# Fourth mixer: the state-space maps and the rotary scores of two heads placed side by side on TensorE's array

## The chip, the cores and the metric

The kernel runs on one NeuronCore of a Trainium2 chip. The metric is the device time of one launch in microseconds (us). PE is TensorE, DVE is VectorE, ACT is ScalarE, POOL is GpSimd, SP is the engine that issues most DMAs. All times below are of one core.

## The reference, cut to what matters

The program is six blocks in a row over 512 positions of width 1024: two mixers of one network, then a second network with mixer, FFN, mixer, FFN. The change lies in the last mixer (the "fourth"), which adds a state-space layer (S5) and latent attention (MLA) side by side:

```python
def odd_mixer_2(t, w_in, ...):
    proj = t @ w_in                      # u (256), c_q (256), c_kv (128), k_r (64)
    y_c = s5_ssm(u, ...)                 # 16 groups of 16 channels, 64 complex states each
    y_d = mla_attention(c_q, c_kv, k_r, ...)   # 6 heads
    return concatenate([y_c, y_d], -1) @ w_out

def s5_ssm(u, ...):
    bu_re = einsum('bsgh,gph->bsgp', ug, bb_re)
    bu_im = einsum('bsgh,gph->bsgp', ug, bb_im)
    x = scan over s of  x_s = ab * x_(s-1) + bu_s        # complex
    y = einsum(x_re, c_re) - einsum(x_im, c_im) + d_skip * ug
    z = gelu(y);  return z * sigmoid(z @ w_glu + b_glu)

def mla_attention(...):
    # per head: 128 plain + 64 rotary columns of q; the rotary key is one for all heads
    sc = (q_nope . k_nope + q_rope . k_rope) * scale
    p = softmax(where(chunk_causal_mask, sc, -inf));  return p @ v
```

## The kernel before, in words

One core runs a single stream of instructions per engine. A framework with tile pools orders each engine's stream when the program is built, by priorities and its own due times; on the chip every stream runs in that order, and a semaphore holds an instruction until what it needs is there. PSUM is eight banks in four pools: P (two banks), Z (three), W (two), O (one). SBUF work tiles come from a pool of 14 tiles of 128x2048 values (`A4`) and one of 13 rows (`U`).

The fourth mixer is `odd2` (line 967). Its stages in order:

- `projT("o2t", ...)` makes `uT`, the 256 S5 channels on partitions: `uT[:, 0]` and `uT[:, 1]`. `projS("o2s", ...)` makes the latents for each of four row blocks; `lat` (line 985) normalises them and transposes them into `CT` and `krT`.
- keys and queries (`kn`, `qn`, lines 1069 to 1087), the rotary part of the queries (`qrT`, up to line 1101) and the values (`va`, line 1108) follow.
- The S5 layer has 8 state tiles. `s5(j, t)` (line 1012) loads a rotation table `tab`, runs two matmuls of 32 contraction rows, `bur` and `bui` (line 1020), and then 14 DVE instructions of 512 columns (lines 1024 to 1033, two of them scans), which end in `sa` (real, line 1030) and `yi` (imaginary, line 1033). `s5_out` (line 1038) maps them to 32 output columns with two matmuls into `py` (lines 1043 and 1044); after four tiles, line 1047 makes `yg`. `s5_step` runs `s5_out` for a tile when the next tile has been written. The tiles 0 to 2 stand before the attention (banks Z), the other five between its heads (banks P).
- `attn(hd)` (line 1116) runs one head: for the four row blocks 1, 2, 3, 0 (256, 384, 512, 128 columns) a plain score matmul of 128 rows (line 1123) and a rotary one of 64 rows (line 1124) into one Z bank `sc`, then `softmax_rows` (memset of the masked corner, DVE maximum, ACT exponential, lines 407 to 411), a DVE reciprocal, an ACT scaling, PE transposes `pw` and an ACT copy into `wt` (line 352). `av2` multiplies by the values (`po`, line 1138).
- The gate of S5 (`zs`, `pp`, `g`, lines 1157 to 1173) ends in `mix(0)` and `mix(1)`, which the output projection `outp` takes last of its eight pieces. `outp` (line 285) also splits the output weights on ACT and DVE (`wb`, `wl`, lines 132 and 115) and adds into eight banks `y`.

Every matmul from FP32 data (scores, `bur`, `bui`, `py`, `po`, transposes over 128 columns aside) is two PE instructions in the trace. In the loop over heads the order is `attn(hd)`, `s5_step(1)`, so one state tile stands beside each head:

Of the kernel before, what the change touches and what calls it, by code (L numbers as in the profile page):

```python
# [12 lines left out]
AF = mybir.ActivationFunctionType  # L13
# [37 lines left out]
class Net:  # L51
# [830 lines left out]
    def s5_setup(self):  # L882
# [61 lines left out]
        for ri in range(2):  # L944
            V.tensor_tensor(w[0], bc[:, ri], b8(fre), ALU.mult)
            V.tensor_tensor(w[1], bc[:, 1 - ri], b8(fim), ALU.mult)
            V.tensor_tensor(w[2], w[0], w[1], ALU.subtract if ri == 0 else ALU.add)
            for jj in range(2):
                pt = self.bank("W", "pbb")
                for c in range(4):  # L950
                    self.nc.tensor.matmul(pt[32 * c : 32 * c + 32, 0:P], lhsT=w[2][:, 4 * jj + c], rhs=self.ident, start=True, stop=True)
                nc.scalar.copy(self.bbT[:, jj, ri], pt[:, 0:P])
# [17 lines left out]
    def odd2(self):  # L970
# [41 lines left out]
        def s5(j, t):  # L1012
            jj, c = j // 4, j % 4
            rs = slice(32 * c, 32 * c + 32)
            tab = self.A4(name="tab")[:, 0:2]
# [3 lines left out]
            for ri, pp in ((0, pr), (1, pi)):  # L1019
                nc.tensor.matmul(pp, lhsT=self.bbT[rs, jj, ri], rhs=uT[rs, jj], start=True, stop=True)  # L1020
            rb = self.rho[:, j : j + 1].to_broadcast([P, S])
            yr, yi, a, b = (self.U(name=n) for n in ("yr", "yi", "sa", "sb"))
            for o, p0, p1, op in ((yr, pr, pi, ALU.add), (yi, pi, pr, ALU.subtract)):
                V.tensor_tensor(a, p0, ct_, ALU.mult)
                V.tensor_tensor(b, p1, st_, ALU.mult)
# [4 lines left out]
            V.tensor_tensor(a, a, b, ALU.subtract)  # L1030
            V.tensor_tensor(yr, yr, st_, ALU.mult)
            V.tensor_tensor(yi, yi, ct_, ALU.mult)
            V.tensor_tensor(yi, yr, yi, ALU.add)
            return a, yi

        py = {}

        def s5_out(j, xr, xi):
            jj, c = j // 4, j % 4
            if c == 0:  # L1040
                py[jj] = self.bank("O", "py")
# [17 lines left out]
        self.s5n = 0  # L1059
        s5_step(1, "Z")  # L1060
# [7 lines left out]
        with self.prio(300):  # L1068
            kn = [self.A4(name="kn") for _ in range(2)]
            qn = [self.A4(name="qn") for _ in range(2)]  # L1070
            va = [self.A4(name="va") for _ in range(2)]
            qrT = self.A4(name="qrT")
            h, l = self.wload("o2kv", 0, 768)
            for hd in range(6):
                ps = self.pb()
                c = slice(hd * P, hd * P + P)
                self.mm3(ps, (h[:, c], l[:, c]), ct(2), True, True)
                nc.scalar.copy(kn[hd // 4][:, hd % 4], ps)
            for pc in range(2):
                h, l = self.wload("o2q", pc, 768)  # L1080
                hv, lv = (t.rearrange("p (k h c) -> p k h c", k=2, h=3) for t in (h, l))
                for g in range(3):
                    hd = 3 * pc + g
                    ps = self.pb()
                    for k in range(2):
                        self.mm3(ps, (hv[:, k, g], lv[:, k, g]), ct(k), k == 0, k == 1)
                    nc.scalar.activation(qn[hd // 4][:, hd % 4], ps, AF.Copy, scale=MLA_SC)
            h, l = self.wload("o2q", 2, 768)
# [26 lines left out]

        def attn(hd):
            r = slice(64 * (hd % 2), 64 * (hd % 2) + 64)
            q, k = qn[hd // 4][:, hd % 4], kn[hd // 4][:, hd % 4]
            wt = self.A4(name="wt")
            for tb in (1, 2, 3, 0):  # L1120
                N = (tb + 1) * P
                ps = self.bank("Z", "sc")
                nc.tensor.matmul(ps[:, :N], lhsT=q[:, tb * P : N], rhs=k[:, :N], start=True, stop=False)  # L1123
                nc.tensor.matmul(ps[:, :N], lhsT=qrT[r, hd // 2, tb * P : N], rhs=krT[r, :N], start=False, stop=True)  # L1124
                e, sm = self.softmax_rows(ps, N)
                rr = self.st(1, "rr")
                V.reciprocal(rr, sm)
                nc.scalar.activation(e[:, :N], e[:, :N], AF.Copy, scale=rr)
                flush()
                self.evac_wt(wt, e, tb)  # L1130
            todo.append(lambda: av2(hd, wt))

# [259 lines left out]
```

## Time and profile before

| | us |
|---|---|
| time, median of three runs (lowest, highest) | 1715.97 (1713.16, 1719.6) |
| the profiled execution's own time | 1708.09 |
| span of the profiled execution | 1706.3 |
| PE busy | 1657.1 (97%) |
| PE weight loads busy | 1318.5 (77%) |
| DVE busy | 964.3 (57%) |
| ACT busy | 669.6 (39%) |
| stretch of the fourth mixer spoken of here | about 1137 to 1340 |

The busy shares are averages over six blocks with different limits. A PE instruction's record is longer than the step to the next one, because matmuls are pipelined; steps between starts are what a stretch costs. Where a view merges several instructions into one row, `x4` is their number.

### The profile page before, as it was taken

How to read it: one execution, taken by the hardware profiler on the slowest of the kernel's cores; microseconds unless marked ns; L12 is line 12 of the kernel's file. 1: busy time of each engine (PE TensorE's matmuls, PEld its weight loads, DVE VectorE, ACT ScalarE, POOL GpSimd, SP SyncE). 2: the span in 40 equal slices, each digit the busy share in tenths (PEclk: the TensorE clock that was granted, in tenths of full speed). 3: DMA queues.
4: the chain of work that ended last, by engine and by line, in shares of the span. 5: the costliest groups of instructions: out<-in, count | busy, mean ns of one | idle time of the engine just before them, and what ended most of it. 6: DMA issues, size and time to landing. Idle time of an engine off the chain costs nothing. (4 is left out here: it accounts for less than half of the span.)

```text
span 1706.3 us, 20536 instructions
## 1 busy us (share of the span) xinstructions
PE 1657.1 (97%) x8008; PEld 1318.5 (77%) x8008; DVE 964.3 (57%) x1824; ACT 669.6 (39%) x1174; POOL 2.0 (0%) x8
## 2 busy tenths in 40 slices
PE   8999999999999998699999999999999999999998
PEld 8657788988789875588888888886447988888886
DVE  7564456765676998763222278468695622224332
ACT  5554234214545246543222244344456422224231
POOL 0000000000000000000000000000000000000000
PEclk8999999999999999799999999999999999999999
DMA  5212243202153220152223235432005323222341
GB/s 204 84 38 74 80 179 117 72 29 99 62 198 115 74 84 1 65 195 101 98 99 99 99 118 196 170 126 78 25 25 197 112 99 99 99 98 89 97 161 50
DMA packets 50241, 175.06 MB, mean 103 GB/s; under 512 B 5584, under 2 KB 6096, under 8 KB 50016
## 3 DMA queue, kind: packets, MB, share of 16 engines
q1 hardware_dynamic: 40896, 142.20, 24.6%
q10 hardware_dynamic: 9216, 31.48, 4.9%
q8 instruction: 63, 1.03, 0.3%
q14 instruction: 34, 0.28, 0.1%
q0 software_dynamic: 32, 0.07, 0.0%
HBM read 156.95 MB, written 16.78 MB: 102 GB/s over the span
## 5 line engine op out<-in xcount | busy, mean ns | idle before, releaser
L115 DVE TENSOR_TENSOR wl<-wr,wh 128x1024 fp32r<-128x1024 f32 (+2 forms) x224 | 271.3, 1213 | 350.4 <-ACT wh L132 335.4
L132 ACT CAST wh<-wr 128x1024 fp32r<-128x1024 f32 (+2 forms) x224 | 233.0, 1042 | 534.8 <-PE pp L147 409.8
L147 PE MATMUL pp<-xl,wh 128*128 128x512 f32 (+1 forms) x1184 | 428.1, 362 | 0.2 <-DVE xl L115 0.2
L144 PE MATMUL pp<-xh,wh 128*128 128x512 f32 (+1 forms) x1184 | 425.2, 361 | 1.2 <-ACT xh L234 1.2
L148 PE MATMUL pp<-xh,wl 128*128 128x512 f32 (+1 forms) x1184 | 425.3, 360 | 0.0
L144 PEld LDWEIGHTS pp<-xh,wh 128*128 128x128 f32 x1184 | 223.6, 190 | 36.1 <-ACT xh L234 2.5
L147 PEld LDWEIGHTS pp<-xl,wh 128*128 128x128 f32 x1184 | 224.4, 190 | 34.0 <-DVE xl L115 1.2
L148 PEld LDWEIGHTS pp<-xh,wl 128*128 128x128 f32 x1184 | 224.4, 190 | 33.7 <-issue 2.3
L147 PE MATMUL pp<-wl,xh 128*128 128x512 f32 (+1 forms) x320 | 126.9, 396 | 0.0
L148 PE MATMUL pp<-wh,xl 128*128 128x512 f32 (+1 forms) x320 | 125.9, 394 | 0.0
L144 PE MATMUL pp<-wh,xh 128*128 128x512 f32 (+1 forms) x320 | 125.9, 393 | 0.0
L144 PE MATMUL y<-wh,ah 128*128 128x512 f32 x288 | 112.5, 390 | 0.0
L147 PE MATMUL y<-wl,ah 128*128 128x512 f32 x288 | 112.3, 390 | 0.0
L148 PE MATMUL y<-wh,al 128*128 128x512 f32 x288 | 112.2, 389 | 0.0
L1189 DVE TENSOR_TENSOR act<-g,pp 128x512 f32<-128x512 f32 x44 | 30.2, 687 | 132.9 <-PE pp L148 131.5
L750 DVE SCALAR_TENSOR_TENSOR ycv<-up,vec,ycv 128x512 f32<-128x512 f32 x120 | 84.4, 740 | 0.4
L144 PEld LDWEIGHTS pp<-wh,xh 128*128 128x128 f32 x320 | 60.2, 188 | 13.9 <-issue 2.6
L147 PEld LDWEIGHTS pp<-wl,xh 128*128 128x128 f32 x320 | 60.2, 188 | 12.9 <-issue 2.4
L148 PEld LDWEIGHTS pp<-wh,xl 128*128 128x128 f32 x320 | 60.3, 188 | 11.1 <-issue 0.6
L321 DVE TENSOR_TENSOR yn<-y,nw 128x512 f32<-128x512 f32 x48 | 31.8, 685 | 58.0 <-ACT yn L319 52.2
L144 PEld LDWEIGHTS y<-wh,ah 128*128 128x128 f32 x288 | 54.1, 188 | 11.5 <-issue 0.4
L148 PEld LDWEIGHTS y<-wh,al 128*128 128x128 f32 x288 | 54.1, 188 | 11.1
(373 smaller groups left out, 2314.0 us busy)
## 6 DMA issues: line engine op xcount, KB each, us to landing
wr<-in_f0gu SPq DMA_DIRECT2D x44, 512.0 KB, 3.3
wr<-in_f1gu SPq DMA_DIRECT2D x44, 512.0 KB, 3.3
wr<-in_f0d SPq DMA_DIRECT2D x22, 512.0 KB, 3.4
wr<-in_f1d SPq DMA_DIRECT2D x22, 512.0 KB, 3.3
xd<-x ACTq DMA_DIRECT2D x20, 512.0 KB, 2.7
x<-xd ACTq DMA_DIRECT2D x20, 512.0 KB, 6.7
wr<-in_o1t SPq DMA_DIRECT2D x16, 512.0 KB, 3.3
nw<-in_nw ACTq DMA_DIRECT2D x12, 512.0 KB, 9.5
```

Source lines behind the costliest of these rows:

```text
L115: return self.nc.vector.tensor_tensor(l, src, h.bitcast(F32), ALU.subtract)
L132: c = nc.scalar.copy(h, raw)
L144: r = mm(out, lhsT=a[0], rhs=b[0], start=first, stop=False)
L147: mm(out, lhsT=a[0], rhs=b[1], start=False, stop=False)
L148: return mm(out, lhsT=a[1], rhs=b[0], start=False, stop=last)
L321: nc.vector.tensor_tensor(yn[j], yb[b][j], postw[j], ALU.mult)
L750: V.scalar_tensor_tensor(y, up[:, j : j + 512], self.v("dw", 4 * j + t), y, ALU.mult, ALU.add)
L1189: nc.vector.tensor_tensor(act[k // 4][:, k % 4], g, ps, ALU.mult)
```

## The change

Five edits, all in the fourth mixer:

- The setup puts the imaginary input map of tile c on the 32 partitions after those of the real one (modulo 128), and two DMAs on POOL's queue copy `uT[:, 0:2]`, shifted by 32 partitions, into `uT[:, 2:4]`. So `bur` and `bui` of a tile read different row groups of the array.
- `s5_out` takes two tiles and issues real, real, imaginary, imaginary; the two tiles write different column groups. It runs when both tiles have been written.
- `attn` takes a pair of heads: two plain scores, then the two rotary scores, on partitions 0 to 63 and 64 to 127, into two banks. Then the two softmaxes. The plain keys and queries of a pair lie in one tile `kq`.
- The loop is over three pairs, with `s5_step(2)` after each.
- `hold` calls give the order-maker two more orders: `bur` of a tile after the last product of the tile before that reads its banks, and the first `py` matmul after the second tile's result. They add no semaphore.

```diff
-                    self.nc.tensor.matmul(pt[32 * c : 32 * c + 32, 0:P], lhsT=w[2][:, 4 * jj + c], ...)
+                    o = 32 * ((c + ri) % 4)
+                    self.nc.tensor.matmul(pt[o : o + 32, 0:P], lhsT=w[2][:, 4 * jj + c], ...)
...
+        nc.gpsimd.dma_start(uT[32:, 2:4], uT[:96, 0:2])
+        nc.gpsimd.dma_start(uT[:32, 2:4], uT[96:, 0:2])
...
-                nc.tensor.matmul(pp, lhsT=self.bbT[rs, jj, ri], rhs=uT[rs, jj], start=True, stop=True)
+                o = 32 * ((c + ri) % 4)
+                r = nc.tensor.matmul(pp, lhsT=self.bbT[o : o + 32, jj, ri], rhs=uT[o : o + 32, 2 * ri + jj], start=True, stop=True)
+                if ri == 0 and self.s5r is not None:
+                    self.hold(r, self.s5r)
...
-            nc.tensor.matmul(py[jj][rs], lhsT=self.s5c[:, 0, j], rhs=xr, start=True, stop=False)
-            nc.tensor.matmul(py[jj][rs], lhsT=self.s5c[:, 1, j], rhs=xi, start=False, stop=True)
+            for n in range(2):
+                for z in two:
+                    o = 32 * (z[0] % 4)
+                    r = nc.tensor.matmul(py[jj][o : o + 32], lhsT=self.s5c[:, n, z[0]], rhs=z[1 + n], start=n == 0, stop=n == 1)
+                    if z is two[0]:
+                        self.hold(r, two[1][3 + n])
...
-            for _ in range(n):
-                if self.s5n < 8:
-                    st.append((self.s5n, *s5(self.s5n, t)))
-                    self.s5n += 1
-                if len(st) > 1 or self.s5n == 8 and st:
-                    s5_out(*st.pop(0))
+            for _ in range(min(n, 8 - self.s5n)):
+                st.append((self.s5n, *s5(self.s5n, t)))
+                self.s5n += 1
+                if len(st) == 2:
+                    s5_out(st)
+                    st.clear()
...
-        def attn(hd):
+        def attn(p):
+            wts = [self.A4(name="wt") for _ in range(2)]
             for tb in (1, 2, 3, 0):
                 N = (tb + 1) * P
-                ps = self.bank("Z", "sc")
-                nc.tensor.matmul(ps[:, :N], lhsT=q[:, tb * P : N], rhs=k[:, :N], start=True, stop=False)
-                nc.tensor.matmul(ps[:, :N], lhsT=qrT[r, hd // 2, tb * P : N], rhs=krT[r, :N], start=False, stop=True)
-                e, sm = self.softmax_rows(ps, N)
+                pss = [self.bank("Z", "sc") for _ in range(2)]
+                for i, ps in enumerate(pss):
+                    last = nc.tensor.matmul(ps[:, :N], lhsT=kq[p][:, 2 + i, tb * P : N], rhs=kq[p][:, i, :N], start=True, stop=False)
+                for i, ps in enumerate(pss):
+                    r = slice(64 * i, 64 * i + 64)
+                    r = nc.tensor.matmul(ps[:, :N], lhsT=qrT[r, p, tb * P : N], rhs=krT[r, :N], start=False, stop=True)
+                    if i == 0:
+                        self.hold(r, last)
+                for ps, wt in zip(pss, wts):
+                    e, sm = self.softmax_rows(ps, N)
...
-        for hd in range(6):
-            attn(hd)
-            s5_step(1, "P")
-            if hd >= 2:
-                self.lo(*late.pop(0))
+        for p in range(3):
+            attn(p)
+            s5_step(2, "P")
+            if p:
+                for _ in range(2):
+                    self.lo(*late.pop(0))
```

The orders of the engines change with it at three places. The first is DVE's row of work where one group of softmax row blocks ends and the next state tile begins. Before (tile 4; `nm` and `rr` are a row block's maximum and reciprocal, `sa`, `sb`, `yr` the tile's):

```order
L1127 RECIPROCAL rr_9797<-nm_9793 128x1
L409 TENSOR_REDUCE nm_9810<-sc_9806 128x1
L1047 SCALAR_TENSOR_TENSOR yg_8994<-uT_8993,vec,py_9396 128x512
L1024 TENSOR_TENSOR sa_9828<-bur_9822,tab_9820 128x512
L1127 RECIPROCAL rr_9814<-nm_9810 128x1
L1025 TENSOR_TENSOR sb_9829<-bui_9823,tab_9820 128x512
L409 TENSOR_REDUCE nm_9852<-sc_9848 128x1
L1026 TENSOR_TENSOR sa_9828<-sa_9828,sb_9829 128x512
```

Now (tile 3, after the last row blocks of the first pair of heads):

```order
L409 TENSOR_REDUCE nm_9732<-sc_9725 128x1
L407 MEMSET sc_9726 64x64
L1142 RECIPROCAL rr_9736<-nm_9732 128x1
L409 TENSOR_REDUCE nm_9746<-sc_9726 128x1
L407 MEMSET sc_9759 64x64
L407 MEMSET sc_9760 64x64
L1142 RECIPROCAL rr_9750<-nm_9746 128x1
L409 TENSOR_REDUCE nm_9766<-sc_9759 128x1
L1142 RECIPROCAL rr_9770<-nm_9766 128x1
L409 TENSOR_REDUCE nm_9777<-sc_9760 128x1
L1031 TENSOR_TENSOR sa_9795<-bur_9789,tab_9787 128x512
```

Before, one tile's products stand between the reductions and reciprocals of one head; now a pair's eight row blocks stand in a row without a product between them, and two tiles follow on each other.

The second place is PE in the attention, at the output maps. Before (tile 4, between the row blocks of the third head):

```order
L1123 MATMUL sc_9947<-kn_9425,qn_9427 128x256
L1124 MATMUL sc_9947<-krT_9109,qrT_9431 128x256
L1043 MATMUL py_9942<-sa_9828,s5c 32x512
L202 MATMUL pw_9882<-cst,e_9877 128x128 x3
L1044 MATMUL py_9942<-yi_9827,s5c 32x512
L1123 MATMUL sc_9970<-kn_9425,qn_9427 128x384
```

Now (tiles 2 and 3, then the first input map of tile 5 and the second pair's scores):

```order
L1052 MATMUL py_9398<-sa_9411,s5c 32x512
L1052 MATMUL py_9398<-sa_9795,s5c 32x512
L1052 MATMUL py_9398<-yi_9410,s5c 32x512
L1052 MATMUL py_9398<-yi_9794,s5c 32x512
L1025 MATMUL bur_9984<-uT_8993,bbT 128x512
L1133 MATMUL sc_9889<-kq_9428 128x384
L202 MATMUL pw_9872<-cst,e_9851 128x128 x2
L1136 MATMUL sc_9888<-krT_9111,qrT_9432 128x384
L1136 MATMUL sc_9889<-krT_9111,qrT_9432 128x384
```

The four output maps now stand in a row, the two rotary scores too, and `bur` of the tile after next stands ahead of them.

The third place is DVE at the end of the attention. Before, tile 7's last sums and the weight splits (`wb`) after them:

```order
L1033 TENSOR_TENSOR yi_10122<-yr_10121,yi_10122 128x512
L407 MEMSET sc_10199 64x64
L115 TENSOR_TENSOR ml_9659<-mo_10159,mh_9657 128x512
L1127 RECIPROCAL rr_10190<-nm_10186 128x1
L409 TENSOR_REDUCE nm_10203<-sc_10199 128x1
L1047 SCALAR_TENSOR_TENSOR yg_8994<-uT_8993,vec,py_9942 128x512
L1127 RECIPROCAL rr_10207<-nm_10203 128x1
L115 TENSOR_TENSOR zs_10227<-yg_8994,zs_10227 128x512
L115 TENSOR_TENSOR wb_10304<-wr_10302,wb_10304 128x1024
```

Now:

```order
L1036 TENSOR_TENSOR sb_10188<-yi_10186,tab_10179 128x512
L115 TENSOR_TENSOR wb_10320<-wr_10318,wb_10320 128x1024
L1037 TENSOR_TENSOR sa_10187<-sa_10187,sb_10188 128x512
L115 TENSOR_TENSOR wl_10326<-wr_10323,wh_10325 128x1024
L1038 TENSOR_TENSOR yr_10185<-yr_10185,tab_10179 128x512
L115 TENSOR_TENSOR wl_10332<-wr_10329,wh_10331 128x1024
L1039 TENSOR_TENSOR yi_10186<-yi_10186,tab_10179 128x512
L115 TENSOR_TENSOR ml_9660<-mo_10215,mh_9658 128x512
L115 TENSOR_TENSOR wl_10338<-wr_10335,wh_10337 128x1024
L1040 TENSOR_TENSOR yi_10186<-yr_10185,yi_10186 128x512
L115 TENSOR_TENSOR ml_9660<-mo_10223,mh_9658 128x512
L1057 SCALAR_TENSOR_TENSOR yg_8994<-uT_8993,vec,py_10006 128x512
```

Seven splits of output weights, three of them above the rows shown, now stand among the 14 instructions of tile 7, ahead of `yg`.

## Rows read from the trace of the kernel before

**Rows 1.** The page, chain of work that ended last: shares of the span by engine.

```profile
PE 30%; ACT 1%; DMA 0%; DVE 0%; issue 0%; ACTq 0%; DVEq 0%
```

**Rows 2.** Windows: start:end, length, busy us of PE, PEld, DVE, ACT, POOL, PEclk, DMA.

```profile
1222.00:1229.00 7.00, 6.08 (x13) 1.80 (x13) 3.93 (x12) 3.69 (x10) 0.00 (x0) 0.76 0.24 78
...
1242.00:1254.40 12.40, 11.78 (x38) 5.31 (x37) 12.14 (x27) 6.19 (x17) 0.00 (x0) 1.00 0.19 49
1254.40:1269.00 14.60, 14.60 (x48) 6.21 (x47) 12.96 (x28) 7.50 (x20) 0.00 (x0) 1.00 0.08 31
...
1282.60:1305.40 22.80, 20.54 (x89) 15.67 (x89) 12.97 (x15) 16.45 (x25) 0.00 (x0) 1.00 0.60 200
```

**Rows 3.** Timeline of DVE: start, us, engine, line, instruction, [idle before].

```profile
1198.73 0.55 DVE L428 TENSOR_TENSOR r<-t,t 128x384 f32<-128x384 f32 x1
...
1213.48 0.68 DVE L1024 TENSOR_TENSOR sa<-bur,tab 128x512 f32<-128x512 f32 x1
...
1242.03 0.67 DVE L1024 TENSOR_TENSOR sa<-bur,tab 128x512 f32<-128x512 f32 x1
...
1269.14 0.67 DVE L1024 TENSOR_TENSOR sa<-bur,tab 128x512 f32<-128x512 f32 x1
...
1271.67 1.22 DVE L1027 TENSOR_TENSOR_SCAN yr<-s5sm,sa 128x512 f32<-128x512 f32 x1
1272.82 0.67 DVE L1025 TENSOR_TENSOR sb<-bur,tab 128x512 f32<-128x512 f32 x1
1273.40 0.68 DVE L1024 TENSOR_TENSOR sa<-bui,tab 128x512 f32<-128x512 f32 x1
...
1274.11 0.69 DVE L1026 TENSOR_TENSOR sa<-sa,sb 128x512 f32<-128x512 f32 x1
...
1282.63 0.75 DVE L1047 SCALAR_TENSOR_TENSOR yg<-uT,vec,py 128x512 f32<-128x512 f32 x1 [0.84 <-PE py L1044]
...
1288.01 2.36 DVE L115 TENSOR_TENSOR wb<-wr,wb 128x1024 fp32r<-128x1024 f32 x2 [0.25 <-ACT wb L132]
```

**Rows 4.** Timeline of PE in earlier mixers: narrow matmuls alone and side by side.

```profile
628.22 1.12 PE L784 MATMUL sc<-kT,qT 64*128 64x512 f32 x2
...
642.39 1.17 PE L784 MATMUL sc<-kT,qT 64*128 64x512 f32 x4
...
81.25 2.38 PE L472 MATMUL po<-wt,sv 128*64 128x512 f32 x16
```

**Rows 5.** Timeline of PE in the attention: values, plain score, transposes, rotary score.

```profile
1246.37 2.42 PE L1138 MATMUL po<-wt,va 128*128 128x512 f32 x8
...
1258.23 1.02 PE L1123 MATMUL sc<-kn,qn 128*128 128x512 f32 x2
1259.09 0.27 PE L202 MATMUL pw<-cst,e 128*128 128x128 f32 x1
1259.30 1.12 PE L1124 MATMUL sc<-krT,qrT 64*128 64x512 f32 x2
```

**Rows 6.** Timeline of PE at the first state tile: input map, projection matmuls.

```profile
1143.62 1.02 PE L1020 MATMUL bui<-uT,bbT 32*128 32x512 f32 x2
1144.57 0.47 PE L144 MATMUL pp<-wh,xh 128*128 128x448 f32 x1
...
1148.72 0.36 PE L148 MATMUL pp<-wh,xl 128*128 128x448 f32 x1
```

**Rows 7.** Timeline of ACT: the copy of `uT`, one row block's exponential.

```profile
1143.39 0.58 ACT L977 COPY uT<-pp 128x512 f32<-128x512 f32 x1
...
1266.99 0.69 ACT L411 ACTIVATE e<-sc,nm 128x512 f32<-128x512 f32 x1
```

**Rows 8.** DMA issues: out<-in, queue, count, KB, median us to landing.

```profile
cst<-in_cst POOLq DMA_DIRECT2D x1, 64.0 KB, 6.3
```

**Rows 9.** Timeline of PE after a pause in the attention.

```profile
1222.92 1.09 PE L1123 MATMUL sc<-kn,qn 128*128 128x256 f32 x2 [1.04 <-ACT e L411]
```

**Rows 10.** Timeline of PE where the output projection takes its last piece.

```profile
1305.40 1.09 PE L144 MATMUL y<-wh,mh 128*128 128x512 f32 x2 [1.34 <-ACT mh L118]
```

More of the change, by code (lines that the diff above doesn't have):

```diff
@@ L950, in s5_setup @@
                 for c in range(4):
-                    self.nc.tensor.matmul(pt[32 * c : 32 * c + 32, 0:P], lhsT=w[2][:, 4 * jj + c], rhs=self.ident, start=True, stop=True)
+                    o = 32 * ((c + ri) % 4)
+                    self.nc.tensor.matmul(pt[o : o + 32, 0:P], lhsT=w[2][:, 4 * jj + c], rhs=self.ident, start=True, stop=True)
                 nc.scalar.copy(self.bbT[:, jj, ri], pt[:, 0:P])
@@ L1024, in s5 @@
                 V.tensor_tensor(a, p0, ct_, ALU.mult)
-                V.tensor_tensor(b, p1, st_, ALU.mult)
+                self.s5r = V.tensor_tensor(b, p1, st_, ALU.mult)
                 V.tensor_tensor(a, a, b, op)
@@ L1029, in s5, with s5_out @@
             V.tensor_tensor(b, yi, st_, ALU.mult)
-            V.tensor_tensor(a, a, b, ALU.subtract)
+            xr = V.tensor_tensor(a, a, b, ALU.subtract)
             V.tensor_tensor(yr, yr, st_, ALU.mult)
             V.tensor_tensor(yi, yi, ct_, ALU.mult)
-            V.tensor_tensor(yi, yr, yi, ALU.add)
-            return a, yi
+            return a, yi, xr, V.tensor_tensor(yi, yr, yi, ALU.add)
         py = {}
-        def s5_out(j, xr, xi):
-            jj, c = j // 4, j % 4
-            if c == 0:
+        def s5_out(two):
+            jj = two[0][0] // 4
+            if two[0][0] % 4 == 0:
                 py[jj] = self.bank("O", "py")
-            rs = slice(32 * c, 32 * c + 32)
-            nc.tensor.matmul(py[jj][rs], lhsT=self.s5c[:, 0, j], rhs=xr, start=True, stop=False)
-            nc.tensor.matmul(py[jj][rs], lhsT=self.s5c[:, 1, j], rhs=xi, start=False, stop=True)
-            if c == 3:
+            for n in range(2):
[4 more added lines that the diff above has]
+                        self.hold(r, two[1][3 + n])
+            if two[1][0] % 4 == 3:
                 y = yg[:, jj]
@@ L1051, in s5_step @@
         def s5_step(n, t):
[L1052 to L1059 removed]
+            for _ in range(min(n, 8 - self.s5n)):
[4 more added lines that the diff above has]
+                    st.clear()
+        self.s5n, self.s5r = 0, None
         s5_step(1, "Z")
@@ L1068, in odd2 @@
         with self.prio(300):
-            kn = [self.A4(name="kn") for _ in range(2)]
-            qn = [self.A4(name="qn") for _ in range(2)]
+            kq = [self.A4(name="kq") for _ in range(3)]
             va = [self.A4(name="va") for _ in range(2)]
@@ L1077, in odd2 @@
                 self.mm3(ps, (h[:, c], l[:, c]), ct(2), True, True)
-                nc.scalar.copy(kn[hd // 4][:, hd % 4], ps)
+                nc.scalar.copy(kq[hd // 2][:, hd % 2], ps)
             for pc in range(2):
@@ L1086, in odd2 @@
                         self.mm3(ps, (hv[:, k, g], lv[:, k, g]), ct(k), k == 0, k == 1)
-                    nc.scalar.activation(qn[hd // 4][:, hd % 4], ps, AF.Copy, scale=MLA_SC)
+                    nc.scalar.activation(kq[hd // 2][:, 2 + hd % 2], ps, AF.Copy, scale=MLA_SC)
             h, l = self.wload("o2q", 2, 768)
@@ L1114, in flush @@
                 todo.pop(0)()
-        def attn(hd):
-            r = slice(64 * (hd % 2), 64 * (hd % 2) + 64)
-            q, k = qn[hd // 4][:, hd % 4], kn[hd // 4][:, hd % 4]
-            wt = self.A4(name="wt")
+        def attn(p):
+            wts = [self.A4(name="wt") for _ in range(2)]
             for tb in (1, 2, 3, 0):
                 N = (tb + 1) * P
-                ps = self.bank("Z", "sc")
-                nc.tensor.matmul(ps[:, :N], lhsT=q[:, tb * P : N], rhs=k[:, :N], start=True, stop=False)
-                nc.tensor.matmul(ps[:, :N], lhsT=qrT[r, hd // 2, tb * P : N], rhs=krT[r, :N], start=False, stop=True)
-                e, sm = self.softmax_rows(ps, N)
[L1126 to L1131, printed above, removed]
+                pss = [self.bank("Z", "sc") for _ in range(2)]
[8 more added lines that the diff above has]
+                    e, sm = self.softmax_rows(ps, N)
+                    rr = self.st(1, "rr")
+                    V.reciprocal(rr, sm)
+                    nc.scalar.activation(e[:, :N], e[:, :N], AF.Copy, scale=rr)
+                    flush()
+                    self.evac_wt(wt, e, tb)
+            for i, wt in enumerate(wts):
+                todo.append(lambda hd=2 * p + i, wt=wt: av2(hd, wt))
         def av2(hd, wt):
```

1 line of the change is left out of this document (removed).

## The prediction

> **What bounds the kernel now.** I read the chain of waits first. It is almost all PE [rows 1], as it must be in a kernel whose PE is busy 97% of its span, and that says little of one stage. So I read the windows of the loop over heads next [rows 2]. In 1242.00 to 1254.40 PE is busy 11.78 of 12.40 us and DVE 12.14; in 1254.40 to 1269.00 PE is busy 14.60 of 14.60 and DVE 12.96. Both engines are full: two heads with their two state tiles take 27.0 us, and DVE alone has 25.1 us of work in them. Whatever PE is spared there, at most 1.9 us in 27 can come off before DVE is the bound. The reader is to see this in the second and third row of that group. The last row shows the other regime: behind the attention (1282.60 to 1305.40) PE is busy 20.54 of 22.80 us and DVE 12.97, so what counts there is how much PE work is left when the gate's operands arrive.
>
> DVE's cost of a state tile follows from its timeline [rows 3]: a scan takes 1.15 us (1271.67 to 1272.82), a product 0.58 (1272.82 to 1273.40), a sum 0.69 (the row at 1274.11). Two scans, eight products and four sums make 9.7 us.
>
> The comparison needs a point that both kernels share. The orders of both have the same PE instruction, at the same place and with the same followers: the first matmul of the output projection's last piece, at 1305.40 [rows 10]. From there on nothing changes, so the change of the time is the shift of that matmul. Upstream I use X, the end of DVE's last rotary step, 1198.73 + 0.55 = 1199.3 [rows 3]. Before, the stages are: X to the first product of tile 3, 14.2; from there to that of tile 5, 28.55; to that of tile 7, 27.1; to the matmul, 36.3 [rows 3, 10].
>
> **Part by part: what PE is spared.** Two scores of 64 rows and 512 columns side by side occupy 1.17 us, one alone 1.12 [rows 4]. Sixteen value matmuls of two heads on two column groups take 2.38 us [rows 4], and eight of one head on full columns 2.42 [rows 5]. So a second narrow matmul beside the first is nearly free, on row groups and on column groups. It must really follow the first, though. In the new order of PE the two input maps are neighbours in 3 of 8 tiles, the output maps form 5 neighbouring pairs out of 8, and the rotary scores 9 pairs of 12 (2688 of 3840 columns); elsewhere another matmul stands between. The rotary pairs spare 2 x 1.12 - 1.17 = 1.07 us for 512 columns, for 2688 columns 5.6. An input map takes 0.95 (1143.62 to 1144.57 [rows 6]), so three spare 2.9. An output map has the same 512 columns and I cost it alike: five spare 4.8. Together 13.3 us of PE time.
>
> **What hides it.** In the loop DVE's work is unchanged, so the gain in the loop is bounded by the 1.9 us above, and it is only had if DVE isn't kept waiting. That is what the second edit decides. Before, one tile's products stand between the row blocks of one head and fill the time in which a row block passes from PE to DVE to ACT and back. Now the eight row blocks of a pair follow each other, and the two tiles come behind them. I replayed DVE's, PE's and ACT's new orders by hand with the durations above.
>
> - **Start.** The imaginary input map of tile 0 now waits for a DMA on POOL's queue. The copy of `uT` ends at 1143.39 + 0.58 = 1143.97 [rows 7], POOL's only other transfer landed after 6.3 us [rows 8], so it is there at 1150.3. PE has 20 projection matmuls ahead of it (4.15 us, 1144.57 to 1148.72 [rows 6]) and reaches it at 1147.8. It stands 2.5 us, with the remaining projection matmuls queued behind and the latents waiting for them. DVE's first tile starts up to 6 us later, under the projection. Bounds for X are -0.4 (one map of 0.95 less, half hidden) and +2.5; I take +1, since the latents' norm and DVE's own backlog hide part.
> - **X to tile 3.** All eight row blocks of the first pair now precede tile 3's first product. They go in four groups of two banks. Of one group of 512 columns the chain is: reduction, like a product, 0.58; exponential 0.69 [rows 7], which frees the bank; the next plain score 0.86 (1258.23 to 1259.09 [rows 5]); two rotary scores 1.17. That is 3.3 us, during which DVE has only two reductions to do. Four groups and the first scores (0.86 x 2 + 1.17) make 16.1; the replay, with ACT's scalings and copies in between, gives 17.0 instead of 14.2: **+2.8**.
> - **Tile 3 to tile 5.** DVE's 25.1 us and the product that makes `yg` (0.65), now in this stretch, and waits: 1.05 for the output maps ahead of `yg` (the imaginary map of tile 3 can only start when DVE has written it, and tile 4 is queued behind `yg` on DVE); 1.0 for an exponential ahead of a reciprocal; and twice the chain from one group of row blocks to the next, 0.69 + 0.86 + 1.17 = 2.7 less the other block's reduction of 0.58, 2.15 each. Sum 32.1 against 28.55; I take 32.0: **+3.45**. PE has new waits here: `bur` of tile 5 waits until DVE has read tile 4's banks, about 4.6 us, with the second pair's scores and transposes queued behind it. DVE is busy with tile 4 for all of this, so I cost it at nothing; if DVE were ahead it would cost up to 4.6.
> - **Tile 5 to tile 7.** The same without `yg` and its wait: 25.1 + 4.3 + 0.6 = 30.0 against 27.1: **+2.9**.
> - **Tail.** Behind tile 7's first product DVE has the tile (9.7), 1.5 of waits for the last exponentials, seven weight splits of 1.18 (two in 2.36 [rows 3]), 8.2, and one more split of 0.6: 20.0 us. Then two output maps one after the other (2.0), `yg` 0.75, gelu and its split 1.1, six gate matmuls with their hand-over 1.6, sigmoid 0.4, and 18 matmuls of the output projection at 20.54/89 = 0.23 each [rows 2], 4.15: 30.0 us, against 36.3: **-6.3**. Before, tile 7 stood in the last head and the tail did much more of PE's work after it. Now that work lies beside tile 7.
>
> **Sum:** 1 + 2.8 + 3.45 + 2.9 - 6.3 = +3.85, about +4 us. The profiled execution took 1708.09 us, so it would take 1712; the median of the runs shown is 7.9 higher, and I predict against the median: 1715.97 + 4 = 1720.0. Bounds of the single terms: X -1.4 to +1.5 about the value taken; the three loop terms 1 each way; the tail 3 each way, since the replay of 24 PE matmuls, ACT and DVE there is the least certain. Added as independent, about 4 each way: 1716 to 1724.
>
> One place where a rule speaks against the change. The rotary pair takes two of the three Z banks at once, and the chain of 2.7 us above runs over a bank that comes free. The Trainium skill, TensorEngine Tiling (Array Packing), Restrictions and Gotchas, says that row tiling raises the pressure on PSUM, since different row tiles write to different banks. The rows agree as far as the 2.15 us of wait are its price; if that pressure cost nothing, the two loop terms would lose 4.3 each and the sum would be about -5.
>
> **Rivals.**
>
> *PE alone sets the end.* If DVE's waits don't come (the row blocks flow and DVE stays 1 to 2 us behind PE all along), the whole of the 13.3 us is gained: 1715.97 - 13.3 = 1702.7. For it: PE is busy 14.60 of 14.60 us in one window. Against: DVE's 25.1 of 27.0 us there [rows 2] would have to be overcome in the tail. Chance 0.11. The Trainium skill, same page, Key Properties, adds that a change of tiling mode drains TensorE, which would make this rival a little larger, since the narrow matmuls stand in fewer groups; the rotary score's 1.12 against the plain one's 1.02 [rows 5] puts that at 0.1 each by the rows.
>
> *TensorE's clock falls in the new waits (the slower side).* After a pause of 1.04 us at 1222.92 [rows 9] the granted clock of 1222 to 1229 is 0.76 [rows 2]: part of that stretch ran at 1.2 GHz and not at 2.4, and (1 - 0.76) x 7.00 = 1.7 us were lost. The new order has at least five places where PE stands longer than that: at tile 0's imaginary map (2.5), among the first pair's row blocks, ahead of `bur` of tile 5 (4.6) and again at tile 7's (2), and ahead of the last output maps. Five falls on the path make 5 x 1.7 = 8.4: +12.3, 1728. It decides if most of these falls land in the softmax chains and the tail, where PE is waited for, and not beneath a state tile on DVE. Chance 0.27. The Trainium skill, TensorE: Matmul & The Clock Gate, Part 1, has the throttled clock as the idle engine's state, which sustained work releases; the row agrees.
>
> *The packing doesn't do what it says.* If the neighbours run one after the other (for one because the two weights come from different partitions), each rotary pair takes 1.05 longer for 512 columns. In the softmax chains, where it lies on the path, that is four groups in the first pair and about two in each of the others, shorter ones among them: some 4 us: +8, 1724. Against it: [rows 4]. Chance 0.08.
>
> **How the numbers follow.** The forecast has 0.54, the rivals 0.11, 0.27 and 0.08. About 0.5% (8.6 us) is what a measurement of this kernel can tell from no change. The first rival is faster by over that: 0.11. The forecast is within it except for 0.06 on the slow side; the clock rival is slower with 0.22 of its 0.27, the third with 0.04 of 0.08. That makes 0.11, 0.57 and 0.32. The range from 1706 to 1731 holds the forecast with its bounds and both slow rivals with 3 us behind the clock's, and leaves out PE alone and rare larger losses, 0.16 in all. The forecast's own range is 1716 to 1724.
>
> **What would show it.** On the steps: X near 1200; tile 3's first product 17 us behind X, tile 5's another 32, tile 7's another 30, with DVE idle ahead of reductions among a pair's row blocks; the last piece's first matmul 30 us behind tile 7's. On the packing: rotary scores merged as `x4` in little more than 1.1 us. On the clock: a PEclk below 1.00 in windows of the attention that had 1.00 before. I am wrong if the first products of tiles 3, 5 and 7 lie as far apart as before or closer, if the tail is as long as before, or if PE's narrow pairs take twice one.

## The result

The changed kernel takes 1728.78 us (median of 6, 1724.33 to 1731.6), the kernel before on the same chip 1717.78. The ratio is 1.0063, with an interval of 1.0035 to 1.0091: some 11 us slower. The profiled execution took 1731.6 us, the highest of the six, and that of before 1708.09, lower than any timed run of its kernel here, so the traces differ by more than the medians. Of the 23.5 us between the two spans 4.8 lie ahead of the first input map, in work that the change leaves alone.

The stages are counted as in the prediction, from the first input map (before 1142.66, after 1147.47) over X, the tiles 3, 5 and 7, to the matmul of [rows 10]. First DVE's timeline after the change, the counterpart of [rows 3] (start, us, engine, line, instruction, idle before):

```profile
1207.10 0.56 DVE L428 TENSOR_TENSOR r<-t,t 128x384 f32<-128x384 f32 x1
...
1228.01 0.68 DVE L1031 TENSOR_TENSOR sa<-bur,tab 128x512 f32<-128x512 f32 x1
...
1261.53 0.68 DVE L1031 TENSOR_TENSOR sa<-bur,tab 128x512 f32<-128x512 f32 x1
...
1297.87 0.68 DVE L1031 TENSOR_TENSOR sa<-bur,tab 128x512 f32<-128x512 f32 x1
...
1320.79 0.75 DVE L1057 SCALAR_TENSOR_TENSOR yg<-uT,vec,py 128x512 f32<-128x512 f32 x1 [1.56 <-PE py L1052]
```

The matmul of [rows 10] now starts at 1329.39. The stages in us:

| | before | after | change | predicted |
|---|---|---|---|---|
| first input map to X | 56.6 | 60.2 | +3.6 | +1 |
| X to tile 3 | 14.2 | 20.35 | +6.15 | +2.8 |
| tile 3 to tile 5 | 28.55 | 33.5 | +5.0 | +3.45 |
| tile 5 to tile 7 | 27.1 | 36.3 | +9.2 | +2.9 |
| tile 7 to that matmul | 36.3 | 31.5 | -4.7 | -6.3 |
| sum | 162.7 | 181.9 | +19.2 | +3.85 |

Windows of the trace after, by these stages (start:end, length, busy us of PE, PEld, DVE, ACT, POOL, then PEclk, DMA share, GB/s), the counterpart of [rows 2]:

```profile
1147.47:1207.66 60.19, 55.67 (x227) 39.30 (x227) 49.83 (x101) 21.10 (x55) 1.00 (x2) 0.94 0.32 102
1207.66:1228.01 20.35, 18.07 (x78) 9.97 (x78) 5.08 (x23) 14.93 (x37) 0.00 (x0) 1.00 0.01 2
1228.01:1261.53 33.52, 25.94 (x86) 10.74 (x85) 26.59 (x56) 13.68 (x37) 0.00 (x0) 0.90 0.10 32
1261.53:1297.87 36.34, 30.52 (x87) 13.01 (x86) 25.71 (x56) 13.74 (x37) 0.00 (x0) 0.77 0.05 15
```

The kernel before has in the two stretches of the loop, tile 3 to 5 and 5 to 7:

```profile
1213.48:1242.03 28.55, 27.16 (x82) 11.24 (x80) 25.13 (x54) 13.04 (x34) 0.00 (x0) 0.94 0.06 19
1242.03:1269.14 27.11, 26.49 (x85) 11.52 (x84) 25.21 (x56) 13.80 (x37) 0.00 (x0) 1.00 0.13 39
```

Two things are to be seen. In the loop, the third and fourth line of the kernel after, DVE has about as much work as before (26.6 and 25.7 us; the first of them now has `yg` too) in longer stretches, so it waits 7 and 10.6 us. And the granted clock is 0.90 and 0.77, where it was 0.94 and 1.00. The two falls of the loop begin where PE resumes after new waits, ahead of `bur` of tiles 5 and 7. PE's timeline (the first row is the wait for the copy of `uT` at the start, the last a pair of rotary scores):

```profile
1153.97 1.09 PE L1025 MATMUL bui<-uT,bbT 32*128 32x512 f32 x2 [1.05 <-DMA uT<-uT]
...
1245.10 1.83 PE L1025 MATMUL bur<-uT,bbT 32*128 32x512 f32 x2 [4.61 <-DVE sb L1032]
...
1276.33 1.21 PE L1025 MATMUL bur<-uT,bbT 32*128 32x512 f32 x1 [1.40 <-DVE sb L1032]
...
1290.46 2.08 PE L1136 MATMUL sc<-krT,qrT 64*128 64x512 f32 x4
```

and the windows around them, same columns as above:

```profile
1241.00:1247.00 6.00, 1.90 (x3) 0.43 (x3) 5.86 (x9) 0.00 (x0) 0.00 (x0) 0.87 0.00 0
1247.00:1253.00 6.00, 6.00 (x13) 2.27 (x14) 5.35 (x13) 3.56 (x10) 0.00 (x0) 0.57 0.00 0
...
1271.00:1277.00 6.00, 2.76 (x8) 0.85 (x9) 5.93 (x10) 0.00 (x0) 0.00 (x0) 0.93 0.22 80
1277.00:1283.00 6.00, 6.00 (x11) 2.01 (x10) 5.21 (x9) 1.69 (x4) 0.00 (x0) 0.50 0.00 0
1283.00:1289.00 6.00, 4.96 (x8) 1.83 (x8) 3.22 (x9) 3.63 (x11) 0.00 (x0) 0.50 0.00 0
1289.00:1295.00 6.00, 5.24 (x20) 2.48 (x18) 1.79 (x7) 2.68 (x8) 0.00 (x0) 0.65 0.01 4
```

From 1241 to 1247 PE works 1.90 us of 6 while DVE is busy 5.86: `bur` of tile 5 waits 4.61 us for DVE, as predicted. Then the clock is at its lower level (1.2 GHz) for most of a window, and PE is "busy" 6.00 of 6.00 with 13 instructions. From 1277 to 1289 it is 0.50 all along: a pair of rotary scores that takes 1.13 us at the full clock (1255.08) takes 2.08 at 1290.46. From 1283 to 1295 DVE is busy 3.22 and 1.79 us of 6. Its timeline there shows that it waits for the softmax chain, which goes over half-speed PE:

```profile
1284.20 0.16 DVE L1142 RECIPROCAL rr<-nm 128x1 f32<-128x1 f32 x1 [1.96 <-ACT e L411]
...
1287.79 0.17 DVE L1142 RECIPROCAL rr<-nm 128x1 f32<-128x1 f32 x1 [1.56 <-ACT e L411]
...
1292.61 0.11 DVE L407 MEMSET sc<- 64x64 f32 x1 [3.25 <-PE sc L1136]
```

The packing itself works. A pair of rotary scores of 512 columns takes what one took (1.12 us [rows 5]):

```profile
1255.08 1.13 PE L1136 MATMUL sc<-krT,qrT 64*128 64x512 f32 x4
```

### The profile page after: what moved, and what is told of

Read it like the earlier page. It is cut to its first block, busy times and chain, and to the rows that moved or that the text cites. A ratio compares the mean times of both kernels' runs of the same rounds, so it can differ in the third digit from the quotient of the medians.

```text
span 1729.8 us, 20550 instructions
## 1 busy us (share of the span) xinstructions
PE 1665.3 (96%) x8008; PEld 1322.6 (76%) x8008; DVE 966.8 (56%) x1824; ACT 669.9 (39%) x1174; POOL 3.0 (0%) x10
## 4 chain that ended last, share of the span: by engine, by line
PE 84%; DVE 8%; ACT 4%; DMA 3%; issue 1%; DVEq 0%; SPq 0%; ACTq 0%
PE pp L144 17%; PE pp L147 17%; PE pp L148 17%; PE y L148 7%; PE y L144 7%; PE y L147 7%; PE pt L202 2%; PE po L359 2%; PE pl L616 1%; PE pw L202 1%; PE sc L1133 1%; PE sc L784 1%; PE sc L1136 1%; PE po L472 1%; DVE wl L115 1%
## 5 line engine op out<-in xcount | busy, mean ns | idle before, releaser
L147 PEld LDWEIGHTS pp<-xl,wh 128*128 128x128 f32 x1184 | 225.4, 190 | 33.5 <-issue 1.0
L144 PEld LDWEIGHTS pp<-wh,xh 128*128 128x128 f32 x320 | 60.2, 188 | 14.7 <-issue 3.4
L147 PEld LDWEIGHTS pp<-wl,xh 128*128 128x128 f32 x320 | 60.2, 188 | 12.9 <-issue 2.4
L148 PEld LDWEIGHTS pp<-wh,xl 128*128 128x128 f32 x320 | 60.2, 188 | 12.0 <-issue 1.3
L321 DVE TENSOR_TENSOR yn<-y,nw 128x512 f32<-128x512 f32 x48 | 31.9, 686 | 58.8 <-ACT yn L319 54.0
```

What stands on the lines that cost most here:

```text
L144: r = mm(out, lhsT=a[0], rhs=b[0], start=first, stop=False)
L147: mm(out, lhsT=a[0], rhs=b[1], start=False, stop=False)
L148: return mm(out, lhsT=a[1], rhs=b[0], start=False, stop=last)
L321: nc.vector.tensor_tensor(yn[j], yb[b][j], postw[j], ALU.mult)
```

## The experiments

Three theories. A: the eight row blocks in a row leave DVE waiting, at any clock. B: PE's new waits bring the clock down, and that is what costs. C: the copy of `uT` at the start is most of it. Times are medians; ratios are to the kernel before on the same chip, with their intervals. Not all runs were on one chip.

**A second look at both kernels** (no edit).

> The kernel before once more, for a second trace. Its runs spread from 1708.7 to 1730.4 us, with mean granted clocks of 0.988 to 0.976. If the spread is the clock in the fourth mixer's attention, this trace shows the same orders and waits, and where its time is above the first trace's 1708 the granted clock of that stretch is lower; if the spread lies elsewhere, the stretch from the first input map to the transposes behind the mixer is 178 to 180 us again.

> The changed kernel once more, for a second trace. Its first trace (1731.6) is the slowest of its runs. Theory A and B: X, tile 3, 5 and 7 at about 60, 80, 113 and 147 to 150 us behind the first input map, with a granted clock below 0.92 in at least one of the two stretches of the loop, longer where it is lower; 1724 to 1731.

The kernel before took 1714.67 us. Its tiles 3, 5 and 7 stand 70.9, 100.5 and 129.7 us behind the first input map (70.8, 99.4 and 126.5 in the first trace), and its windows from tile 3 to 5 and 5 to 7 are:

```profile
1216.02:1245.60 29.58, 28.19 (x81) 11.61 (x80) 25.25 (x54) 12.53 (x33) 0.00 (x0) 0.88 0.06 19
1245.60:1274.81 29.21, 28.59 (x86) 11.76 (x84) 25.04 (x56) 14.30 (x38) 0.00 (x0) 0.94 0.11 36
```

Same order, same work, but 0.88 and 0.94 where the first trace has 0.94 and 1.00, and 3.1 us more. So the clock in this loop already moves the kernel before, and the first trace was a lucky one. The changed kernel took 1732.01, with 33.8 and 36.3 us for the two stretches at 0.85 and 0.77: its falls came back. From the first input map to the matmul of [rows 10] the second traces take 166.9 and 181.8 us, +14.9 instead of +19.2. Both traces of the kernel before are faster than its median and both of the changed kernel slower than its own, so the traces overstate the 11 us.

**The first edit alone**: input maps and the copy of `uT`.

```diff
-                    self.nc.tensor.matmul(pt[32 * c : 32 * c + 32, 0:P], ...)
+                    o = 32 * ((c + ri) % 4)
+                    self.nc.tensor.matmul(pt[o : o + 32, 0:P], ...)
...
+        nc.gpsimd.dma_start(uT[32:, 2:4], uT[:96, 0:2])
+        nc.gpsimd.dma_start(uT[:32, 2:4], uT[96:, 0:2])
...
-                nc.tensor.matmul(pp, lhsT=self.bbT[rs, jj, ri], rhs=uT[rs, jj], start=True, stop=True)
+                o = 32 * ((c + ri) % 4)
+                nc.tensor.matmul(pp, lhsT=self.bbT[o : o + 32, jj, ri], rhs=uT[o : o + 32, 2 * ri + jj], start=True, stop=True)
```

> The kernel before with only the first edit: imaginary input maps on the neighbouring row group and the two DMAs that copy uT. Theories A and B: only the start is late, by the 3.6 us by which the last rotary step was late in the changed kernel, less one to three input maps of 0.95: 1718 to 1722. Theory C: most of the 11 us is here, 1725 to 1729.

1714.86 us, ratio 0.9972 (0.9946 to 0.9999): a little faster, below what A and B expected, and C falls. X comes 59.7 us behind the first input map, 3.1 late, nearly as in the changed kernel; the two stretches of the loop get 0.8 and 1.5 shorter than in the first trace before, and from tile 7's first product to `yg` it is 0.7.

**The same without the wait for the copy**: tile 0 keeps its imaginary map on the old row group, from a small weight tile of its own.

```diff
+            if ri == 1:
+                self.bb0 = self.cst_p.tile([32, P], F32, name="bb0")
...
+                self.nc.tensor.matmul(pt[0:32, 0:P], lhsT=w[2][:, 0], rhs=self.ident, start=True, stop=True)
+                nc.scalar.copy(self.bb0, pt[0:32, 0:P])
...
+                if j == 0 and ri == 1:
+                    nc.tensor.matmul(pp, lhsT=self.bb0, rhs=uT[0:32, 0], start=True, stop=True)
...
```

> As the first-edit-only kernel (1714.9), but tile 0's imaginary input map stays on the row group of its real one, from an extra 32x128 weight tile, so nothing waits for the copy of uT at the start. If the late start is on the path: the last rotary step comes at 56.6 us behind the first input map again (59.7 with the wait) and the time falls by 2 to 3 us, 1711 to 1713. If the projection's PE work hides it: 1714 to 1716.

1712.6 us, ratio 0.9977 (0.9962 to 0.9991): faster than the kernel before, by 0.2%. X is back at 56.3. In the traces the 3.4 us are still there at tile 7's first product (123.9 us behind the first input map, 127.35 with the wait, at the same clocks), so up to there the late start was on the path. The times don't tell the two kernels apart: 2.3 us in the medians, nothing by the ratios. The loop, tile 3 to 5 and 5 to 7:

```profile
1215.16:1242.90 27.74, 26.27 (x84) 10.77 (x82) 25.26 (x54) 13.25 (x35) 0.00 (x0) 0.94 0.06 20
1242.90:1268.56 25.66, 24.98 (x86) 10.79 (x84) 24.95 (x56) 14.02 (x37) 0.00 (x0) 1.00 0.12 42
```

In the second line DVE is busy 24.95 of 25.66 us. The 1.9 us that the prediction named as all that PE can give in such a stretch are mostly used up by this edit alone: 27.1 has become 25.66.

**The copy in halves**, in the changed kernel.

```diff
             nc.scalar.copy(uT[:, i], ps)
+            nc.gpsimd.dma_start(uT[32:, 2 + i], uT[:96, i])
+            nc.gpsimd.dma_start(uT[:32, 2 + i], uT[96:, i])
...
-        nc.gpsimd.dma_start(uT[32:, 2:4], uT[:96, 0:2])
-        nc.gpsimd.dma_start(uT[:32, 2:4], uT[96:, 0:2])
```

> The changed kernel with the copy of uT cut in two halves that are issued right after each half is written, so the first tile's half can land earlier. Theories A and B: the first imaginary map starts 1 to 3 us earlier and the time falls by 0 to 3 us, 1725 to 1729. Theory C: the time falls to 1718 to 1721.

1726.99 us, ratio 1.0047 (1.0023 to 1.0071). The first imaginary map starts 1.9 us behind the real one instead of 6.5, X comes at 58.8 instead of 60.2. The time is in the range that A and B gave; a gain over the changed kernel is not clear of the noise (the intervals overlap).

**The output maps of two tiles alone**: `s5_out` and `s5_step` as changed, one head and one tile in turn.

> The kernel before with only the output maps of two tiles together; heads single, one state tile beside each head. Theory A and B: the heads keep DVE and PE busy, the neighbouring maps spare up to 4.8 us of PE: 1712 to 1718. If the wait of the first map for the second tile's result alone makes the pauses that lower the clock: 1720 to 1726.

1724.32 us, ratio 1.0025 (0.9998 to 1.0052): unclear against no change, but not the gain that was expected. Its trace is of the slowest of its ten runs (1732.54); the two stretches of the loop take 32.8 us each there, at 0.81 and 0.82. Its windows ahead of tile 3's first product (1219.78) and behind it:

```profile
1208.79:1214.79 6.00, 6.00 (x22) 2.84 (x20) 0.95 (x5) 4.82 (x12) 0.00 (x0) 1.00 0.00 0
1214.79:1220.79 6.00, 6.00 (x15) 2.73 (x15) 2.63 (x9) 3.44 (x10) 0.00 (x0) 0.64 0.26 87
1220.79:1226.79 6.00, 6.00 (x12) 2.84 (x13) 4.06 (x7) 1.22 (x4) 0.00 (x0) 0.50 0.01 3
```

The clock falls although PE has no pause at all in these 18 us; what it did just before the fall were two input maps of 32 rows, transposes and scores of 64 rows. B in its simple form, that it takes a pause, does not hold.

**The paired heads alone**: `attn(p)`, `kq` and the loop over pairs as changed, maps and `uT` as before.

> The kernel before with only the paired heads: plain and rotary scores of two heads, eight row blocks in a row, two state tiles after each pair; input and output maps and uT as before. Theory A: the loop is as long as in the changed kernel, 1723 to 1730. Theory C: under 1720. Theory B: the loop is long only where the granted clock is below 0.9; since the input maps of a tile are still held up by the tile before, 1722 to 1730, with PEclk of 0.75 to 0.9 in the loop.

1728.84 us, ratio 1.0064 (1.0039 to 1.0088): as slow as all five edits together.

**The paired heads, not side by side**: each head's rotary score right behind its plain one.

```diff
...
-                for i, ps in enumerate(pss):
                     r = slice(64 * i, 64 * i + 64)
-                    r = nc.tensor.matmul(ps[:, :N], lhsT=qrT[r, p, tb * P : N], rhs=krT[r, :N], start=False, stop=True)
-                    if i == 0:
-                        self.hold(r, last)
+                    nc.tensor.matmul(ps[:, :N], lhsT=qrT[r, p, tb * P : N], rhs=krT[r, :N], start=False, stop=True)
```

> The paired heads alone (1728.8) with each head's rotary score right behind its plain score, so that no two rotary scores are neighbours; all else in the same order. If packing does what it says and the chain runs over it: 4 to 8 us slower than with the pairs, 1732 to 1737. If DVE and the clock set the loop and the packing gains nothing there: 1726 to 1731. If side by side narrow matmuls are not faster here: 1728 or less.

1726.78 us, ratio 1.0044 (1.0015 to 1.0074): no slower than with the packing. X to tile 3, tile 3 to 5 and 5 to 7 of the packed kernel, then of this one:

```profile
1203.41:1221.74 18.33, 17.97 (x73) 9.13 (x72) 6.32 (x25) 14.09 (x36) 0.00 (x0) 1.00 0.00 0
1221.74:1260.36 38.62, 32.91 (x88) 12.77 (x86) 26.37 (x57) 14.10 (x37) 0.00 (x0) 0.78 0.08 28
1260.36:1297.42 37.06, 31.68 (x87) 12.51 (x86) 25.69 (x55) 13.73 (x37) 0.00 (x0) 0.82 0.04 15
```

```profile
1204.07:1224.24 20.17, 19.92 (x75) 9.76 (x74) 6.17 (x27) 14.46 (x36) 0.00 (x0) 1.00 0.00 1
1224.24:1259.70 35.46, 31.37 (x87) 12.71 (x86) 26.23 (x56) 13.83 (x36) 0.00 (x0) 0.86 0.08 30
1259.70:1295.20 35.50, 31.77 (x87) 12.74 (x86) 25.25 (x55) 13.73 (x37) 0.00 (x0) 0.86 0.04 15
```

At the full clock, in the first line of each, the packing is worth 1.84 us. In the loop of these two traces it is given back: with it the clock stands at 0.78 and 0.82, without it at 0.86.

**State tiles between a pair's row blocks**, in the changed kernel.

```diff
                     self.evac_wt(wt, e, tb)
+                if tb in (2, 0):
+                    s5_step(1, "P")
...
             attn(p)
-            s5_step(2, "P")
```

> The changed kernel with one thing undone: within a pair of heads one state tile is issued after the first four row blocks and one after the last four, instead of both after all eight. Maps, rotary pairs and the copy of uT stay as changed. Theory A (the eight row blocks in a row leave DVE waiting, and that stretches the loop): the first products of tiles 3, 5 and 7 lie within 29 us of each other again, DVE's waits ahead of reciprocals and memsets in the loop fall from some 20 us to under 6, and the time is 1706 to 1718. Theory B (the loss is the clock that falls while PE waits for tile banks): these waits stay, the granted clock of the loop stays below 0.9, the time stays above 1724. Theory C (the loss is the copy of uT at the start): no change against the changed kernel, 1725 to 1731.

1725.27 us, ratio 1.0045 (1.0020 to 1.0070), some 3 us below the changed kernel, with overlapping intervals. X to tile 3 is 12.2 instead of 20.35, but the loop keeps its clock falls:

```profile
1217.58:1251.42 33.84, 28.35 (x95) 11.42 (x93) 26.72 (x58) 15.15 (x39) 0.00 (x0) 0.90 0.09 32
1251.42:1283.19 31.77, 27.58 (x80) 12.21 (x81) 25.61 (x56) 13.42 (x36) 0.00 (x0) 0.84 0.05 17
```

and the tail, 40.9 us at a clock of 0.87, loses more than the change had gained there. So A, as stated, falls: the order within the pair is not all.

**Input maps without the wait, paired heads, tiles between the row blocks, output maps tile by tile**: the form in which paired scores had the best case.

> The input maps on neighbouring row groups without the wait for the copy (the 1712.6 kernel), plus paired heads with one state tile after each half of a pair, and output maps tile by tile as before. If paired rotary scores can pay at all, this is the form: 1706 to 1711. If the pair's softmax chain over three banks costs more than the packing spares, as in the interleaved kernel (1725.3): 1717 to 1725.

1722.85 us, ratio 1.0036 (1.0006 to 1.0067), with 0.89 in both stretches of the loop. Against the 1712.6 of the same kernel with single heads, pairing heads costs 10 us here.

**Useless work against the clock**, in the changed kernel, in two versions: one ahead of the output maps of tiles 2/3 and of 4/5, one ahead of 4/5 alone (shown).

```diff
+            if two[0][0] == 4:
+                pf = self.bank("W", "fill")
+                for n in range(5):
+                    nc.tensor.matmul(pf, lhsT=self.ident, rhs=uT[:, 0], start=True, stop=True)
```

> The changed kernel plus ten useless matmuls of 512 columns (0.86 us each, 8.6 us of PE work, result read by nobody): five ahead of the output maps of tiles 2/3 and five ahead of those of 4/5, where PE stands still; the value matmuls thereby stand behind the output maps and cover part of the wait of the next tile's input map. Theory B (part of the loss is the clock that falls after these pauses): the granted clock from tile 3 to tile 7, 0.90 and 0.77 in the changed kernel, rises above 0.93, the stretch from tile 3 to tile 7 shortens from 69.9 us to 62 to 65, and the time is 1720 to 1725 although PE does more. Theory A alone (DVE's waits on the softmax chain, at any clock): the stretch stays within 2 us or grows, 1727 to 1733.

> The changed kernel with five useless matmuls of 512 columns (4.3 us of PE work) ahead of the output maps of tiles 4/5 only; the place ahead of tiles 2/3, where they held up the gate's first half, is left as changed. Theory B: the granted clock from tile 5 to tile 7 is 1.00 instead of 0.77, that stretch is 31 us instead of 36.3, and the time falls by 3 to 6 us: 1722 to 1726. If the clock there doesn't matter for the end: 1727 to 1732.

With both, 1728.22 us (four runs), ratio 1.0072 (1.0052 to 1.0091): the first filler held up the output maps, and `yg` waited 4.17 us instead of 1.14. Tile 3 to 7 took 67.5 us, not 62 to 65. With the second alone 1725.49, ratio 1.0050 (1.0023 to 1.0078). Tile 3 to 5 and 5 to 7 of the latter:

```profile
1226.43:1259.71 33.28, 25.71 (x86) 11.02 (x85) 26.57 (x56) 13.66 (x37) 0.00 (x0) 0.90 0.10 32
1259.71:1290.66 30.95, 26.79 (x97) 11.38 (x96) 25.81 (x56) 13.63 (x37) 0.00 (x0) 1.00 0.05 18
```

In tile 5 to 7 PE is given 4.3 us of work that nobody reads, the clock stays at 1.00, and the stretch takes 30.95 us instead of 36.3 (30.96 with both fillers). From `bur` of tile 7 to tile 7's first product it is 15.0 us instead of 21.5, and DVE's wait for the rotary scores of 512 columns is

```profile
1285.42 0.11 DVE L407 MEMSET sc<- 64x64 f32 x1 [1.04 <-PE sc L1140]
```

where it was 3.25. So B holds for this stretch: what the fall costs there is about 5.4 us. Why the clock stayed up is less clear, since the filler also moves the pair's value matmuls: they start 7.7 to 15.7 us behind tile 5's first product instead of 2.3 to 7.9, next to the output maps, and `bur` of tile 7 no longer waits. No run parts the filler's own work from this new order. Less than that arrives at the end: 3.3 us in the medians, 2.2 by the ratios, with overlapping intervals.

## Why the prediction was right, and where it was off

The direction and the range (1706 to 1731) held; the likeliest value, 1720.0, was 8.8 us low, and the forecast's own range, 1716 to 1724, missed. No clear change had 0.57; what came, slower by more than 8.6 us, had 0.32. The time is that of the second rival (1728), and it is the room made for that rival that held the result, not the forecast's sum: in the traces all five stages came out longer than forecast.

- **What bounds the loop: right.** DVE's 25 us per pair of heads are the floor. The input maps alone bring a stretch to 25.66 us with 24.95 of DVE work, and there is hardly anything left for rotary scores to give.
- **Start: mis-sized.** +1 was taken, +3.6 measured. The chain of waits of the trace after has it (start, us, what):

```profile
1149.09 4.75 DMA uT<-uT
1153.97 1.11 PE bui L1025 x2
```

  `bui` started 6.5 us behind `bur`, and DVE's first tile waited for it:

```profile
1155.10 0.69 DVE L1032 TENSOR_TENSOR sb<-bui,tab 128x512 f32<-128x512 f32 x1 [5.21 <-PE bui L1025]
```

  The copy landed 4.7 us after its issue, not 6.3, and PE stood 1.05 us, not 2.5: what was costed too low is DVE. I took it that DVE's backlog hides most of the late first tile; against the kernel without the wait 3.4 us reach X in the traces. The clock, 0.94 in this stretch, is little of it: the kernel with the output maps alone, which doesn't copy `uT`, has 0.94 there as well, and X at 57.35.
- **X to tile 3: mis-sized.** 17.0 was replayed, 20.35 measured, at a clock of 1.00, so this is the chain alone. The replay names scalings and copies on ACT, but not the table load of 1.28 us there, the value copies `va` between the exponentials, or tile 3's two input maps, and it has the two rotary scores of each group side by side. The chain of waits after the change has the load and the maps, and the scores of 512 columns one behind the other:

```profile
1211.76 1.28 ACT L411
...
1218.21 1.05 PE bur L1025 x2
...
1220.64 1.05 PE sc L1136 x2
1222.17 1.05 PE sc L1136 x2
1223.64 1.05 PE bui L1025 x2
```

  With the paired heads alone, where those two scores run together, it is 18.33. How the 3.35 us divide, no run shows. DVE's timeline shows the wait for the first exponential:

```profile
1213.65 0.16 DVE L1142 RECIPROCAL rr<-nm 128x1 f32<-128x1 f32 x1 [3.62 <-ACT e L411]
```

- **The loop: the chain right, the clock costed at nothing.** At a clock of 1.00 tile 5 to 7 takes 30.95 us, 30.0 was forecast. With the clock as it is, 36.3. Tile 3 to 5 was forecast at 32.0, measured 33.5 at 0.90. The step that failed is to cost PE's new waits at nothing because DVE is busy meanwhile, which the forecast says of the 4.6 us ahead of `bur` of tile 5 and takes over for the next stretch. DVE is busy; but the waits are followed by half a clock in the next softmax chain, where PE is waited for. The stretch with the wait of 4.61 us came out 1.5 us over its forecast. The dear one is the next, 6.3 over: PE waits 1.38 and 0.75 us at the output maps of tiles 4/5 and 1.40 ahead of `bur` of tile 7, and then the clock is at 0.50 from 1277 to 1289 and at 0.65 up to 1295.
- **The clock rival: right in kind, wrong in count.** It had five falls of 1.7 us. The trace shows fewer and longer ones: (1 - 0.90) x 33.5 = 3.4 and (1 - 0.77) x 36.3 = 8.4 us of full-clock work lost in the two stretches of the loop, against 1.7 before [rows 2, 9]. Not all that is lost is paid for: of the 8.4 the filler gave back 5.4. [rows 9] shows a fall behind a pause of 1.04 us, and the new order has one of 4.6: that spoke for more than 0.27.
- **Tail: right in kind**, -4.7 instead of -6.3, at a clock of 1.00.
- **What PE is spared: too much.** The rotary scores came out as 9 pairs and the input maps as 3. Of the output maps, in tiles 0/1, 2/3 and 4/5 only one couple each ran together, the second tile's real map with the first one's imaginary map (in 2/3 both at 1238.12), since the first real map doesn't wait for the second tile, and in 6/7 none: 3, not 5. And little of it mattered where DVE or the chain sets the pace.

The rival that PE alone sets the end is out, since the time rose, and so is the one that the packing fails, since the pairs take what one takes. What is shown of the cause: the paired heads alone bring a loss as large as the change's, with the rotary scores side by side or not (11 and 8 us by the ratios, overlapping), and in one stretch of the traces the clock makes 5.4 us. How the 11 us divide between the order and the clock stays open.

## What to carry to other kernels

Before work is taken off an engine, look whether another one is as full in the same stretch; here 1.9 us in 27 were to be had, and a small edit took 1.4 of them. If an edit brings work into groups to pack it, count what the grouping does to the engine that was fed by the old interleaving, and to the granted clock in the stretches where the packed engine now stands. A wait that is free for the busy engine isn't free if the waiting one comes back at half its clock.

## What the runs showed of the hardware

- TensorE's clock can fall without a pause: 0.64 and 0.50 in two windows in which PE is busy 6.00 of 6.00 us, with narrow maps, transposes and scores in them. In the kernel before almost the same sequence, at 1207 to 1220, ran at 1.00. What tells the two apart stays open; no run tried to. The Trainium skill, TensorE: Matmul & The Clock Gate, Part 1, has the throttled clock as the idle engine's state. The fall at `bur` of tile 5, after 4.61 us of waiting, agrees; the one in these two windows doesn't, and the measurement decides.
- Useless matmuls can pay: 4.3 us of them, with the new order that they brought, shortened a stretch by 5.4 us.
- The kernel before spreads by its clock. Of 75 of its runs the 32 with a mean granted clock of 0.984 or more average 1713.8 us, the 23 with 0.979 or less 1724.7. All six of the changed kernel have 0.976 to 0.980 and average 1728.5: at like clocks it is some 4 us slower. That is a comparison of groups of runs, not an experiment, and that it is also the forecast's sum is chance: stage by stage X to tile 3 alone is 6.15 us longer at a clock of 1.00.
- Whether the edits add up, these runs can't tell. Alone, the input maps give 3 us in the medians (5 by the ratio), the output maps cost 7 (4 by the ratio, with an interval from nothing), the paired heads 11; together they cost 11. The medians sum to 15, the ratios to 10.5, and each interval is about 4 us or more either way.
